# Removal key's inverse norm in a recurrent mixer: token-major power on GpSimd and four transposes, in place of logarithm and exponential on ScalarE

## The chip, the cores and the metric

One core of one Trainium2 chip runs the whole kernel. Its engines work side by side, each through its own queue in order: TensorE (PE: matrix products into PSUM), VectorE (DVE), ScalarE (ACT), GpSimd (POOL, which does not touch PSUM here) and SyncE (SP, which issues the weight loads). The metric is the device time of one execution in microseconds (us). The three timed runs gave 1562.68, 1556.77 and 1562.52 us: median 1562.52 us.

## The reference, cut to what matters

Two layers of attention branches are followed by two layers of a second kind. In each of these, three mixers work on the same input of 256 tokens and 1024 features: gated linear attention, an RWKV-7 recurrence (4 heads of 64 features) and sparse attention; an output projection, a layer norm and a feed-forward network follow. The change is in the recurrence, in the normalised key that the state forgets by (the removal key `kk`):

```python
kk = (k * k_k).reshape(B, S, H, N)                      # H = 4 heads, N = 64
kk = kk / jnp.maximum(jnp.sqrt(jnp.sum(kk * kk, axis=-1, keepdims=True)), 1e-12)
...
xs = (heads(r), heads(decay), heads(k), heads(v),
      (-kk).transpose(1, 0, 2, 3), (kk * a_h).transpose(1, 0, 2, 3))
def step(state, inp):
    r_t, w_t, k_t, v_t, a_t, b_t = inp
    sa = jnp.einsum('bhvk,bhk->bhv', state, a_t)
    state = (state * w_t[:, :, None, :] + sa[..., None] * b_t[:, :, None, :]
             + v_t[..., None] * k_t[:, :, None, :])
    return state, jnp.einsum('bhvk,bhk->bhv', state, r_t)
```

## The kernel before, in words

Feature-major tiles hold 256 features as 128 partitions x 2 column groups x 256 tokens, so that a partition's two groups belong to two different heads and a head covers 64 partitions. The recurrence (`rwkv`, line 897) is worked out in closed form over chunks, not step by step. For the norm (lines 939 to 952) ACT squares `k * k_k` in two halves (L941), PE multiplies each half by `c_ones64`, a 128x128 matrix of two blocks of ones, which leaves each head's sum on all its 64 partitions (L944), DVE clips it at 1e-24 (L946), ACT takes the logarithm (L947) and the exponential of minus half of it (L949), and DVE multiplies the key by the result (L952, whose records carry L301, the line of the helper `stt`). In the trace the squares' tile is `kk`, the clipped sum and its inverse root `ssg`, the normalised key `kn`.

From `kn` DVE makes the operands of the recurrence (`r_AR`, `r_B`, `ke`, `r_K`: lines 954 to 970). PE sums r x k per head (L975) and later starts the chunk's triangular inverse (L1014).

The four streams of a layer (recurrence, gated linear attention, direct and compressed sparse attention) are generators that `side_by_side` (line 210) draws from in turn by the numbers that they yield. Each instruction gets a priority, shifted by the table `AHEAD`; a scheduler then writes one fixed order for each engine, so that the recurrence's instructions stand between those of the others. In the stretch of the norm these are

- L353: the projection of the gated linear attention, 128x512 products in full fp32 (two records each in the trace);
- L656 and L659: scores of the direct attention and their mask; L595, L597, L601: row maximum, its negative and the exponentials; L446: transposes of the probabilities (and of everything else that `transposed` turns over); L610: their copy to `ptsb`; L613: the weighing of the values by them; L438: a filler product;
- L1356 to L1382: the compressed attention's hidden layer. Its PSUM bank (`psg`, one buffer) is free for L1379 only when DVE has made `n_hid` (L1372).

PE's order and each other engine's are fixed when the kernel is built; at run time an engine waits at the head of its queue until its operands are there. PSUM for the recurrence comes from `psr`, a pool of one pair of banks that are handed out in turn.

A power on GpSimd stands elsewhere already: L890 (128x8, in `head_norm`), L479 and L499 (128x1, in the row norms).

Of the kernel before, what the change touches and what calls it, by code (L numbers as in the profile page):

```python
# [8 lines left out]
F32 = mybir.dt.float32  # L9
F32R = mybir.dt.float32r  # L10
BF16 = mybir.dt.bfloat16
AF = mybir.ActivationFunctionType
ALU = mybir.AluOpType
# [138 lines left out]
class Kern:  # L152
    def __init__(self, ctx, tc, ap):
        self.tc, self.nc, self.ap = tc, tc.nc, ap
        pool = lambda n, b, **k: ctx.enter_context(tc.tile_pool(name=n, bufs=b, **k))
        self.cp = pool("const", 1)
        self.wh = pool("whi", 4)
        self.wl = pool("wlo", 4)
        self.wr = pool("raw", 5)
        self.sm = pool("small", 4)  # L160
        self.pp, self.pr = (pool(n, 1, space=PSUM) for n in ("pp", "pr"))
        self.rest = {}
        self.turn = 0
        self.last = self.pr
        self.slot = 0
        nc = self.nc
        self.c = {}
        const = lambda n, w, v: (lambda t: (nc.vector.memset(t, v), t)[1])(self.cp.tile([128, w], F32, name=n))
        self.one = const("one", 1, 1.0)
        self.mhalf = const("mhalf", 16, -0.5)  # L170
        self.ln10 = const("ln10", 1, float(10 * np.log(2.0)))
        warm = self.cp.tile([128, 1], F32, name="warm")
        nc.scalar.activation(warm, self.one, AF.Square)

# [722 lines left out]
    def rwkv(self, l, R, wa, g0, tl, P, hp, rows, out):  # L897

        nc = self.nc
        mm = nc.tensor.matmul  # L900
        r, k, v = R["r"], R["k"], R["v"]
        cst = self.c
# [26 lines left out]
        if l:  # L929
            tv = self.tanh_half(self.low_rank(self.psr, P, P_TAIL, 32, 64, tl), hp[:, 4:6])  # L930
            d = self.c3("vd")
# [7 lines left out]
        sq = self.c3("kk2")  # L939
        for c in range(2):  # L940
            nc.scalar.activation(sq[:, c], k[:, c], AF.Square, scale=P[:, P_KK + c:P_KK + c + 1])  # L941
        ss = self.psr(2, 256)
        for c in range(2):
            mm(ss[:, c], cst["ones64"], sq[:, c], start=c == 0, stop=c == 1)  # L944
        sg = self.c3("ssg")
        nc.vector.tensor_scalar(sg, ss, 1e-24, None, op0=ALU.max)  # L946
        nc.scalar.activation(sg, sg, AF.Ln, scale=float(2.0 ** 20))  # L947
        rn = sg
        nc.scalar.activation(rn, sg, AF.Exp, scale=-0.5, bias=self.ln10)  # L949
        kn = self.c3("kn")  # L950
        for c in range(2):
            self.stt(kn[:, c], k[:, c], P[:, P_KK + c:P_KK + c + 1], rn[:, c], ALU.mult, ALU.mult)  # L952
# [19 lines left out]
        for tt in range(2):  # L972
            for c in range(2):
                o = 4 * tt + 2 * c
                mm(bp[:, o:o + 2], rk[:, c, 128 * tt:128 * tt + 128], P[:, P_RK + 2 * c:P_RK + 2 * c + 2],  # L975
                   start=tt == 0 and c == 0, stop=tt == 1 and c == 1)
# [35 lines left out]
        for n, j, b in quads:  # L1012
            tt, c = tiles[n]
            mm(ps[half[b], j, n], ar4[tt][half[j], 0, c, half[b]], Bt[half[j], c, 128 * tt + 64 * b:128 * tt + 64 * b + 64],  # L1014
               start=n == 0, stop=n == 3)
# [44 lines left out]
        for q in range(1, 6):  # L1060
            ps, idle = pair()
            for n, j, b in quads:
                tt, c = tiles[n]
# [30 lines left out]
        for tt in both:  # L1094
# [4 lines left out]
            for h in range(4):  # L1099
                j, c = hh(h)  # L1100
# [3 lines left out]
            for h in range(4):  # L1104
                j, c = hh(h)
# [3 lines left out]
            for h in range(4):  # L1109
                j, c = hh(h)  # L1110
# [11 lines left out]
        for h in range(4):  # L1122
            j, c = hh(h)
# [22 lines left out]
        for tt in range(2):  # L1146
            yield 3
            tm, M, WU, V = tiles[tt]
            if tt:
                pw = self.psr(2, 128)  # L1150
                for h in range(4):
                    j, c = hh(h)
# [4 lines left out]
            for h in range(4):  # L1157
                j, c = hh(h)
# [327 lines left out]
    def block2_layer(self, l, xT):  # L1486
# [48 lines left out]
        def rwkv():  # L1535
            for t in self.rwkv(l, R, wa, g0, tl, P, hp, rows, yr):
                yield t
            with self.sec("ofr"):
                feats["r"] = self.out_feat([yr[:, 0], yr[:, 1]], 0.5, self.psr)

        self.side_by_side([(0, "rwkv", rwkv()), (AHEAD["t_gla"], "gla", gla()), (AHEAD["t_dir"], "nsa", direct()), (AHEAD["t_cmp"], "cmp", compressed())])
        with self.sec("h1"):
            for n in range(2):
# [257 lines left out]
```

## Time and profile before

| what | us |
|---|---|
| three timed runs | 1562.68, 1556.77, 1562.52 (median 1562.52) |
| the profiled execution's own time | 1556.73 |
| its span | 1554.9 |
| PE busy | 1492.6 (96%) |
| PE weight load busy | 1286.2 (83%) |
| DVE busy | 938.9 (60%) |
| ACT busy | 710.6 (46%) |
| POOL busy | 50.0 (3%) |

The span is the profiled execution from its first to its last record; 1.8 us of its own time lie around it. Busy times are sums over instructions, and PE's ends are modelled, so its share says where PE had work, not that it ran at its peak. The granted clock is a share of full speed (2.4 GHz); its mean over the span is 0.988. The two stretches of the norm lie at about 775 to 790 us (first layer) and 1205 to 1220 us (second layer).

### The profile page before, as it was taken

The page shows a single profiled execution, that of the slowest core. Times are in us where ns is not written, and L with a number is a line of the kernel's source. Part 1 is how long each engine was busy: PE and PEld are TensorE (multiplying, and loading weights), DVE is VectorE, ACT ScalarE, POOL GpSimd, SP SyncE. Part 2 cuts the span into 40 slices and gives each one's busy share as a digit, 9 for nine tenths or more (in the row PEclk, how much of TensorE's full clock was granted, in tenths as well). Part 3 has the DMA queues.
Part 4 walks back from the last instruction along what each step waited for, and adds up shares of the span by engine and source line. Part 5 has one row for each costly group of instructions (what it writes and reads, how often), then busy time and mean ns, then how long its engine had stood idle before and what let it go on. Part 6 is the DMA issues. An engine that isn't in the chain of part 4 may idle for free.

```text
span 1554.9 us, 26032 instructions
## 1 busy us (share of the span) xinstructions
PE 1492.6 (96%) x10502; PEld 1286.2 (83%) x10502; DVE 938.9 (60%) x1531; ACT 710.6 (46%) x1286; POOL 50.0 (3%) x82
## 2 busy tenths in 40 slices
PE   6999999999999999999999989999999999899997
PEld 5877899988787999868767769998888677789986
DVE  5586565565686655565367475556754675755564
ACT  5545554445454444444454334444454544344451
POOL 0000000000000000000011010000000010100000
PEclk9999999999999999999999999999999999999999
DMA  7743435445444445556710245556447101445560
GB/s 254 235 147 122 150 122 189 158 156 180 166 149 131 149 136 182 167 152 201 249 34 2 80 142 176 188 172 224 139 146 254 42 1 42 144 164 191 181 215 27
DMA packets 72984, 231.69 MB, mean 149 GB/s; under 512 B 8736, under 2 KB 11552, under 8 KB 72864
## 3 DMA queue, kind: packets, MB, share of 16 engines
q1 hardware_dynamic: 67248, 219.74, 42.8%
q10 hardware_dynamic: 5616, 10.30, 2.1%
q8 instruction: 82, 1.34, 0.3%
q14 instruction: 38, 0.31, 0.1%
HBM read 228.96 MB, written 1.05 MB: 148 GB/s over the span
## 4 chain that ended last, share of the span: by engine, by line
PE 46%; DVE 4%; DMA 3%; ACT 2%; issue 1%; POOL 0%; DVEq 0%; ACTq 0%; SPq 0%
PE ps L357 10%; PE ps L355 10%; PE ps L356 10%; PE ps L353 4%; DMA raw<-in_stream_dram 2%; PE ps L446 2%; PE ps L1258 2%; PE ps L613 1%; PE ps L656 1%; DVE wlo L298 1%; ACT whi L321 1%; PE ps L438 1%; PE ps L867 1%; PE ps L1052 0%; PE ps L1001 0%
## 5 line engine op out<-in xcount | busy, mean ns | idle before, releaser
L298 DVE TENSOR_TENSOR wlo<-raw,whi 128x1024 fp32r<-128x1024 f32 (+2 forms) x364 | 428.1, 1183 | 313.3 <-ACT whi L321 306.2
L321 ACT CAST whi<-raw 128x1024 fp32r<-128x1024 f32 (+2 forms) x364 | 367.8, 1018 | 403.9 <-PE ps L356 206.4
L355 PE MATMUL ps<-xTh,whi 128*128 128x256 f32 x720 | 205.5, 285 | 4.4 <-ACT whi L321 4.4
L357 PE MATMUL ps<-xTh,wlo 128*128 128x256 f32 x720 | 205.5, 285 | 1.5 <-DVE wlo L298 1.5
L356 PE MATMUL ps<-xTl,whi 128*128 128x256 f32 x720 | 205.1, 285 | 0.0
L357 PE MATMUL ps<-hTh,wlo 128*128 128x256 f32 x640 | 182.4, 285 | 0.0
L355 PE MATMUL ps<-hTh,whi 128*128 128x256 f32 x640 | 181.7, 284 | 0.0
L356 PE MATMUL ps<-hTl,whi 128*128 128x256 f32 x640 | 181.5, 284 | 0.0
L355 PEld LDWEIGHTS ps<-xTh,whi 128*128 128x128 f32 x720 | 138.8, 193 | 6.1 <-ACT whi L321 4.8
L357 PEld LDWEIGHTS ps<-xTh,wlo 128*128 128x128 f32 x720 | 138.8, 193 | 2.0 <-DVE wlo L298 1.9
L356 PEld LDWEIGHTS ps<-xTl,whi 128*128 128x128 f32 x720 | 138.7, 193 | 0.8
L356 PEld LDWEIGHTS ps<-hTl,whi 128*128 128x128 f32 x640 | 122.6, 191 | 1.1 <-issue 0.7
L355 PEld LDWEIGHTS ps<-hTh,whi 128*128 128x128 f32 x640 | 122.6, 192 | 0.7
L357 PEld LDWEIGHTS ps<-hTh,wlo 128*128 128x128 f32 x640 | 122.6, 192 | 0.4 <-issue 0.3
L355 PE MATMUL ps<-whi,hTh 128*128 128x512 f32 (+2 forms) x256 | 97.3, 380 | 1.1 <-ACT wi L772 1.1
L357 PE MATMUL ps<-whi,hTl 128*128 128x512 f32 (+2 forms) x256 | 97.0, 379 | 0.0
L356 PE MATMUL ps<-wlo,hTh 128*128 128x512 f32 (+2 forms) x256 | 95.9, 375 | 0.8 <-DVE wlo L298 0.8
L355 PE MATMUL ps<-whi,xTh 128*128 128x512 f32 (+1 forms) x144 | 55.1, 383 | 4.0 <-ACT xTh L425 2.5
L355 PEld LDWEIGHTS ps<-whi,hTh 128*128 128x128 f32 x256 | 48.1, 188 | 11.8 <-issue 3.3
L355 PE MATMUL ps<-whi,f_h 128*128 128x512 f32 x144 | 57.1, 396 | 0.0
L356 PE MATMUL ps<-wlo,f_h 128*128 128x512 f32 x144 | 57.0, 396 | 0.0
L357 PE MATMUL ps<-whi,f_l 128*128 128x512 f32 x144 | 56.9, 395 | 0.0
(474 smaller groups left out, 2898.1 us busy)
## 6 DMA issues: line engine op xcount, KB each, us to landing
raw<-in_stream_dram SPq DMA_DIRECT2D x346, 512.0 KB, 4.2
raw<-in_stream_dram SPq DMA_DIRECT2D x56, 256.0 KB, 3.1
whi<-in_stream_dram SPq DMA_DIRECT2D x11, 512.0 KB, 5.9
wlo<-in_stream_dram SPq DMA_DIRECT2D x11, 512.0 KB, 6.5
row<-in_ln_w_dram ACTq DMA_DIRECT2D x8, 256.0 KB, 4.0
row<-in_ln_b_dram ACTq DMA_DIRECT2D x8, 256.0 KB, 4.6
raw<-in_stream_dram SPq DMA_DIRECT2D x4, 480.0 KB, 3.8
raw<-in_stream_dram SPq DMA_DIRECT2D x4, 420.0 KB, 5.4
```

The lines of the kernel that those rows point to most:

```text
L298: self.nc.vector.tensor_tensor(out=out, in0=a, in1=b, op=op)
L321: nc.scalar.copy(hi[:, :b - a], raw)
L353: mm(out, a, b, start=start, stop=stop)
L355: mm(out, a[0], b[0], start=start, stop=False)
L356: mm(out, a[0], b[1], start=False, stop=False)
L357: mm(out, a[1], b[0], start=False, stop=stop)
L438: self.nc.tensor.matmul(o, self.negb, self.causb[:, None, :].to_broadcast([128, n, 128]), start=True, stop=True)
L446: self.nc.tensor.transpose(pt[:, j], s, self.ident)
L613: nc.tensor.matmul(o[:, ocol(h)], ps[:, i * nk + k, :], vt(k, h), start=first and i == 0 and k == 0, stop=last and i == nh - 1 and k == nk ...
L656: nc.tensor.matmul(s3[:, i], qT[pr, h // 2], kT(pr, h, 128 * nk), start=i == 0, stop=False)
L867: self.nc.tensor.matmul(ps[:, c], P[r0:r1, off + 128 * c:off + 128 * c + 128], rhs[r0:r1], start=c == 0, stop=c == 1)
L1258: mm(ps[:, tt, c], a, e, start=tt + c == 0, stop=c == 1 and (tt == 1 or m == 128))
```

## The change

The squares stay feature-major. PE now takes them as the stationary operand, 128 tokens at a time, against two columns of `c_ones64` (the first of each block): four products of 128x2, which leave the heads' sums token-major, 128 tokens x (2 token tiles x 2 groups x 2 heads) = 128x8. DVE clips these 8 columns, POOL raises them to the power -0.5 in one 128x8 instruction, DVE spreads each of the values over 64 columns in two copies of 128x256 into the tile of the squares, and four transposes on PE bring that back to feature-major, into a PSUM bank (`rn`), from which DVE multiplies the key. The logarithm, the exponential, the tile `ssg` and the constant `ln10` go.

```diff
-        self.ln10 = const("ln10", 1, float(10 * np.log(2.0)))
...
-        ss = self.psr(2, 256)
+        ss = self.psr(2, 2, 2)
+        for tt in range(2):
+            for c in range(2):
+                mm(ss[:, tt, c], sq[:, c, 128 * tt:128 * tt + 128], cst["ones64"][:, ::64], start=tt + c == 0, stop=tt + c == 2)
+        s8 = self.sm.tile([128, 2, 8], F32, name="r_s8")
+        nc.vector.tensor_scalar(s8[:, 0], ss.rearrange("p t c j -> p (t c j)"), 1e-24, None, op0=ALU.max)
+        nc.gpsimd.tensor_tensor(out=s8[:, 1], in0=s8[:, 0], in1=self.mhalf[:, 0:8], op=ALU.pow)
+
+        rn = self.psr(2, 256)
+        for tt in range(2):
+            wide = sq[:, tt].rearrange("p (c j d) -> p c j d", c=2, j=2)
+            nc.vector.tensor_copy(wide, s8[:, 1, 4 * tt:4 * tt + 4].rearrange("p (c j) -> p c j", c=2)[:, :, :, None].to_broadcast([128, 2, 2, 64]))
         for c in range(2):
-            mm(ss[:, c], cst["ones64"], sq[:, c], start=c == 0, stop=c == 1)
-        sg = self.c3("ssg")
-        nc.vector.tensor_scalar(sg, ss, 1e-24, None, op0=ALU.max)
-        nc.scalar.activation(sg, sg, AF.Ln, scale=float(2.0 ** 20))
-        rn = sg
-        nc.scalar.activation(rn, sg, AF.Exp, scale=-0.5, bias=self.ln10)
+            for tt in range(2):
+                nc.tensor.transpose(rn[:, c, 128 * tt:128 * tt + 128], sq[:, tt, 128 * c:128 * c + 128], self.ident)
         kn = self.c3("kn")
```

In the changed file the helpers' lines stand one lower (L445 is the transposes' L446, L612 the weighing's L613, L352 the projection's L353), the new sums are L944, the new clip L946, the power L947, the copies L952, the transposes L955, and lines behind them stand six higher.

PE in the first layer, from the new sums to the weighing, before:

```order
L446 MATMUL ps<-c_ident,pexp 128x128 x4
L944 MATMUL ps<-kk_7914,c_ones_6935 128x256
L353 MATMUL ps<-whi,xTf 128x512
L656 MATMUL ps<-n_kw,n_qT 128x128
L613 MATMUL ps<-n_vs_7043,ptsb 128x64 x4
L1364 MATMUL ps<-c_fold,n_Xl 128x30 x2
L656 MATMUL ps<-n_kw,n_qT 128x128
L944 MATMUL ps<-kk_7914,c_ones_6935 128x256
L656 MATMUL ps<-n_kw,n_qT 128x128 x2
...
L438 MATMUL ps<-causb,negb 128x512
L446 MATMUL ps<-c_ident,pexp 128x128 x4
```

The same place on PE in the changed kernel (`kk` is the squares' tile under L944 and the spread inverse norm under L955):

```order
L445 MATMUL ps<-c_ident,pexp 128x128 x4
L944 MATMUL ps<-c_ones_6933,kk_7912 128x2
L352 MATMUL ps<-whi,xTf 128x512 x2
L612 MATMUL ps<-n_vs_7041,ptsb 128x64 x4
L1370 MATMUL ps<-c_fold,n_Xl 128x30 x2
L944 MATMUL ps<-c_ones_6933,kk_7912 128x2 x3
L655 MATMUL ps<-n_kw,n_qT 128x128 x4
...
L437 MATMUL ps<-causb,negb 128x512
L955 MATMUL ps<-c_ident,kk_7912 128x128
L445 MATMUL ps<-c_ident,pexp 128x128
L955 MATMUL ps<-c_ident,kk_7912 128x128 x3
L1385 MATMUL ps<-n_hidk,P_7022 128x32 x2
```

The four scores L656 stand together behind the sums now, and the new transposes stand in the filler's and the probabilities' wake, five rows (with mask and filler) behind the last sum; one more projection product stands ahead of the sums, and L1379 (now L1385) moves up to right behind the transposes. In the second layer the order is the same but for two probability transposes, not one, between the first new transpose and the other three.

DVE in the second layer, before:

```order
L298 TENSOR_TENSOR yn<-ps,n_cf 128x512
L946 TENSOR_SCALAR ssg<-ps 128x512
L1367 TENSOR_SCALAR n_x_11999<-n_x_11999 128x60
L595 TENSOR_REDUCE mx<-ps 128x4
L298 TENSOR_TENSOR n_x_11999<-n_x_11999,ps 128x60
L597 TENSOR_SCALAR nb<-mx 128x4
```

And in the changed kernel:

```order
L297 TENSOR_TENSOR yn<-ps,n_cf 128x512
L946 TENSOR_SCALAR r_s_12020<-ps 128x8
L1373 TENSOR_SCALAR n_x_12004<-n_x_12004 128x60
L952 COPY kk_12012<-r_s_12020 128x256
L297 TENSOR_TENSOR n_x_12004<-n_x_12004,ps 128x60
L952 COPY kk_12012<-r_s_12020 128x256
L594 TENSOR_REDUCE mx<-ps 128x4
L300 SCALAR_TENSOR_TENSOR n_hidv<-n_x_12004,ps 128x4x15
L300 SCALAR_TENSOR_TENSOR kn<-r_k,P_11114,ps 128x256 x2
L596 TENSOR_SCALAR nb<-mx 128x4
```

The copies, which wait for POOL, stand ahead of the row maximum and, in the second layer, one of them ahead of the product for `n_x`; in the first layer that product stands ahead of both copies. No instruction of the weight stream stands between the clip and the copies.

ACT in the first layer, before:

```order
L1366 ACTIVATE n_x_7906<-ps 128x60
L947 ACT_TABLE_LOAD
L947 ACTIVATE ssg<-ssg 128x512
L1369 ACT_TABLE_LOAD
L1369 ACTIVATE n_x_7906<-n_x_7906 128x60
L949 ACTIVATE ssg<-ssg,ln_80 128x512
L601 ACTIVATE pexp,n_den<-ps,nb 128x128 x4
L1382 ACTIVATE n_kc<-ps 64x15 x2
```

And in the changed kernel:

```order
L1372 ACTIVATE n_x_7904<-ps 128x60
L1375 ACTIVATE n_x_7904<-n_x_7904 128x60
L1388 ACTIVATE n_kc<-ps 64x15 x2
L600 ACTIVATE pexp,n_den<-ps,nb 128x128 x4
```

Two table loads and two activations of 128x512 go in each layer; no other table load of the program moves.

## Rows read from the trace of the kernel before

**Rows 1.** Windows, both stretches: length, busy (count) per engine, granted clock, DMA share, GB/s.
```profile
770.00:800.00 30.00, 30.00 (x160) 18.42 (x159) 12.54 (x26) 17.14 (x49) 3.55 (x8) 1.00 0.22 70
1200.00:1230.00 30.00, 30.00 (x192) 18.64 (x190) 15.51 (x30) 17.71 (x50) 2.79 (x6) 1.00 0.16 55
```

**Rows 2.** Chain that ended last, first layer: start us, us on the chain, what.
```profile
772.58 1.09 PE ps L656 x8
...
776.80 0.43 PE ps L944 x2
777.24 0.86 PE ps L353 x2
778.10 0.42 PE ps L656 x2
778.51 1.03 PE ps L613 x8
779.55 0.42 PE ps L1364 x4
779.96 0.42 PE ps L656 x2
780.38 0.63 PE ps L944 x2
781.01 0.64 PE ps L656 x4
781.65 0.32 PE ps L659
781.97 0.22 PE ps L438
782.18 0.44 PE ps L446 x4
...
789.08 0.84 PE ps L613 x8
...
794.26 0.79 PE ps L975 x8
...
825.29 0.84 PE ps L1229 x8
```

**Rows 3.** Timeline of ACT: start us, us, line, operation.
```profile
780.24 1.28 ACT L947 ACT_TABLE_LOAD   x1
...
786.85 0.59 ACT L610 COPY ptsb<-ps 128x512 f32<-128x512 f32 x1
```

**Rows 4.** Timeline of POOL: powers of 128x8.
```profile
880.31 1.68 POOL L890 TENSOR_TENSOR hn<-hn,mhalf 128x8 f32<-128x8 f32 x1 [49.63 <-DVE hn L889]
...
898.94 2.57 POOL L890 TENSOR_TENSOR hn<-hn,mhalf 128x8 f32<-128x8 f32 x1 [4.95 <-DVE hn L889]
```

**Rows 5.** Timeline of DVE: the clip, the products behind it, and beside the powers.
```profile
781.05 0.69 DVE L946 TENSOR_SCALAR ssg<-ps 128x512 f32<-128x512 f32 x1 [0.60 <-PE ps L944]
...
791.47 0.69 DVE L298 TENSOR_TENSOR ke<-r_r,ke 128x512 f32<-128x512 f32 x1
...
880.07 0.17 DVE L889 TENSOR_SCALAR hn<-hn 128x8 f32<-128x8 f32 x1
880.39 0.69 DVE L298 TENSOR_TENSOR n_t<-ps,n_cf 128x512 f32<-128x512 f32 x1 [0.16 <-PE ps L613]
...
898.76 1.22 DVE L298 TENSOR_TENSOR wlo<-raw,whi 128x1024 fp32r<-128x1024 f32 x1
```

**Rows 6.** Groups by line and form: busy us, mean ns | idle before.
```profile
L1103 DVE COPY r_WU<-ps 64x256 f32<-64x256 f32 x2 | 0.8, 418 | 1.6 <-PE ps L1102 1.6
...
L479 POOL TENSOR_TENSOR rs<-ms,mhalf 128x1 f32<-128x1 f32 x10 | 5.5, 552 | 539.3 <-DVE ms L477 539.3
```

**Rows 7.** Windows, second layer behind the norm, columns as in rows 1.
```profile
1230.00:1246.00 16.00, 13.77 (x154) 10.35 (x146) 12.39 (x34) 5.36 (x16) 1.40 (x2) 1.00 0.10 34
1246.00:1254.00 8.00, 7.33 (x25) 4.79 (x26) 4.20 (x11) 4.25 (x9) 1.09 (x1) 0.57 0.00 0
```

## The prediction

> **What bounds the kernel now.** I read the page first (PE is busy nearly all the span, every other engine far less), then the place of the change: the windows of the two stretches, the chain of waits through them, the timelines of ACT, DVE and POOL there, and last the windows of the clock. In both stretches, 30 us each, PE is busy 30.00 of 30.00 us at the full granted clock, ACT 17 to 18, DVE 13 to 16, POOL about 3 [rows 1]. The chain of waits agrees: from the first sum (776.80 us) to the weighing (789.08) and on to L975 (794.26) it stays on PE without a gap [rows 2]. So in this stretch a microsecond counts only if PE does more or less work, or if PE is made to wait. What ACT saves counts only through an operand that PE waits for, and PE waits for none here.
>
> **What ACT loses.** Two table loads in each layer, of 1.28 us as the first of them [rows 3], and the logarithm and exponential with them. PE is on the chain throughout, so I price all of it at nothing. What hides it is the projection L353, of which PE still has eight pieces after the first probabilities. If that cover were gone, the copy L610, which ends at 786.85 + 0.59 = 787.44, 1.6 us ahead of its reader at 789.08 [rows 2, 3], would be the first to profit.
>
> **PE's own work, per layer.** Between the first sum and the probability transposes PE does, besides the projection, L944 0.43 + 0.63, L656 0.42 + 0.42 + 0.64, L613 1.03, L1364 0.42, L659 0.32 and L438 0.22: 4.53 us [rows 2]. In the new order the sums are four products of two columns. Their nearest row is L1229, the same form, eight records in 0.84. The scores stand in one piece as at 772.58 (1.09), and L613 no longer follows a score: 0.84 as at 789.08 [rows 2]. With L1364, L659 and L438 as they are: 0.84 + 1.09 + 0.84 + 0.42 + 0.32 + 0.22 = 3.73, so 0.80 less. The four transposes cost what four cost at 782.18, 0.44 [rows 2]. Net PE work: -0.36 us. Most of that saving is the order's (scores no longer split in three), not the smaller sums'.
>
> **The new wait, per layer.** PE now meets transposes that depend on a trip through three engines. From the end of the last sum: 0.04 us to DVE (L944's end at 781.01, the clip's start at 781.05 [rows 2, 5]), the clip of eight columns 0.17 as L889, 0.07 to POOL (880.24 to 880.31), the power 1.68 [rows 4, 5], 0.04 back, the first copy of 256 columns 0.42 as L1103 [rows 6], 0.05 to PE: 2.47 us. What PE has in the meantime is the scores, mask and filler: 1.09 + 0.32 + 0.22 = 1.63 us. PE stands for 0.84 us. Then the second copy: its result is some 0.3 us behind the first's, PE has one (first layer) or two (second) probability transposes and its own in between, 0.11 each; in the second layer a product for `n_x` also stands between the copies. I put 0.14 on it in both. Stall 0.98, work -0.36: +0.62 us per layer, **+1.2 us** for both.
>
> What is queued behind: on PE everything, since its order is fixed, the probability transposes and then L353. On DVE the row maximum and `n_hidv` wait behind the copies, which wait for POOL; L1379 needs `n_hidv`'s bank, and it now stands right behind the transposes. The tanh in front of `n_hidv` is no longer behind two table loads, so I count it in time, at nothing; if it isn't, PE waits a few tenths.
>
> **The power's price** is the one that decides. Two durations of the 128x8 form stand in the trace, 1.68 and 2.57 [rows 4]; the 128x1 form takes 0.55 [rows 6]. Beside the long one DVE was in the middle of `wlo` (128x1024, from 898.76), beside the short one it worked on `n_t`, with one operand in PSUM [rows 5]. In the new order nothing of the weight stream stands between clip and copies; beside the power DVE has a small product and then waits. So I take 1.68, and keep both ends: at 0.55 the whole trip (1.34 us) lies under the 1.63 and the layer gains 0.36; at 2.57 the stall is 1.87 and the layer loses 1.51. For two layers: -0.7 to +3.0 us.
>
> The Trainium skill ("SBUF — State Buffer", section "Who interferes with whom") states that a DVE instruction with two SBUF inputs and a GpSimd instruction that reads SBUF exclude each other for the whole instruction. The pair of rows agrees (2.57 beside `wlo`, 1.68 beside `n_t`), and by that rule too the new power is a short one, because the DVE product beside it reads PSUM.
>
> The skill's "GPSIMD Engine Reference" (section "Elementwise — side-by-side cycle accounting") has GpSimd about half as fast as VectorE on a two-input elementwise operation. By that the power would be an estimated 0.34 us, twice the clip's 0.17, and the trip would be hidden; the trace's 1.68 speaks against it, ten times the clip, so the sum goes by the trace and the rule's outcome is the first rival below.
>
> **Behind the stretch.** PE would reach the first transpose at 776.80 + 3.73 + 1.72 (two projection products at 0.86, one more than before) + 0.84 = 783.09, and the weighing that needs L610 after the transposes of both kinds (0.88), 0.14, L1379 (about 0.4) and eight projection pieces (8 x 0.43): 787.95. L610 ended at 787.44 before, and I expect it within a few tenths of that: its exponentials lose the wait for the tables and gain one for the copies. L975 is then reached at 787.95 + 0.84 + 3.44 = 792.23 instead of 794.26, since two products moved behind it. Its operand was ready at 791.47 + 0.69 = 792.16 [rows 5]. I take no wait, but there is no cushion left: should DVE run half a microsecond later, it is +0.5 per layer, +1.0 in all.
>
> All else shifts with PE: there is no gap in the chain to absorb it, and I see no transfer that limits this stretch (DMA share 0.22 and 0.16 [rows 1]).
>
> **Rivals.**
>
> 1. *Hidden.* The power is fast enough, or the order leaves more cover than I count. For it: POOL is idle and DVE quiet. Against it: no 128x8 power shorter than 1.68 in the rows shown. Price -0.7 us: 1561.8.
> 2. *The clock.* Behind the second layer's norm the granted clock was 0.57 over eight microseconds [rows 7]: most of them at the lower level (1.2 GHz), after 16 us in which PE was busy for 13.77 only, at full clock. Full-speed work lost there: 8 x (1 - 0.57) = 3.4 us. That stretch now begins somewhat later, and the dip may not come: +1.2 - 3.4 = -2.2, so 1560.3. The three runs of one program, 5.9 us apart, show that something of this size comes and goes anyway.
> 3. *Slower.* The power takes its long form in both layers, PE idles 1.9 us per layer ahead of the stretch in which it has gaps anyway, and the clock falls once more in each layer: 3.0 + 2 x 3.4 = +9.8 us, 1572.3. For it: the dip after a stretch with gaps [rows 7]. Against it: PE is at 30.00 of 30.00 around the new wait, and a gap of one to two microseconds stands alone there. It decides from a power of about 2.5 us on.
> 4. *The change doesn't do what it says:* the loads come back elsewhere. The order shows four fewer and no new one, so this is all but excluded; it would cost ACT, not PE: still +1.2.
>
> **How the numbers follow.** The sum is made against the profiled execution (own time 1556.73 us, span 1554.9), which stands with the lowest of the three runs (1556.77) and 5.8 us below their median. +1.2 makes 1557.9 there, and on the median 1562.52 + 1.2 = 1563.7 us, which I give. Chances: the forecast 0.60, hidden 0.12, the clock's gain 0.14, slower 0.10, other 0.04. The range: from a run at the lower level with the trip hidden (1556.77 - 0.7 = 1556.1, a little less for its own spread) to the long powers and late L975 with half a dip on top (1562.68 + 3.0 + 1.0 + 1.7 = 1568.4, a little more): 1555.5 to 1569. Half a per cent, about what a measurement of this kernel can tell from no change, is 7.8 us. The forecast and rivals 1 and 2 lie within it; faster by more would need two dips to vanish together (0.06); rival 3 makes slower, less the part in which it costs under 7.8 (0.09); the same 0.85.
>
> **What would show it.** In the changed kernel's chain: the new sums eight records in 0.84 and the scores one piece in 1.09; a gap on PE of 0.7 to 1.1 us ahead of the first L955 in both layers, released by DVE's copy, and that by a POOL record of about 1.7 us; ACT without table loads there; L975 reached within 0.5 us of its operand. I am wrong if PE has no gap there (the trip is hidden), if the gap is near 2 us (the long power), if L975 or L1379 shows a wait above half a microsecond, or if the time moves by more than 4 us with the granted clock unchanged.

## The result, and the profile after

The changed kernel takes 1566.53 us on the median of 20 runs (1557.19 to 1572.40); the kernel before, run beside it, 1555.67 (20 runs, 1551.49 to 1562.68). The ratio is 1.0062, 95% interval 1.0046 to 1.0079: slower by 7 to 12 us. A second measurement, in another session, gave 1.0039 (1.0010 to 1.0068). The forecast was +1.2 us, 1563.7 us on the median. The 1566.53 us lie within the forecast range of 1555.5 to 1569, but only because the 1562.52 us to which the +1.2 was added were high: over 20 runs the kernel before took 1555.67.

| | before | after |
|---|---|---|
| profiled execution's own time, us | 1556.73 | 1562.58 |
| its span, us | 1554.9 | 1560.8 |
| mean granted clock of the span | 0.988 | 0.982 |
| PE busy, us | 1492.6 | 1500.3 |
| ACT busy, us | 710.6 | 704.2 |

Where the norm stands, the profile after looks as forecast. First the windows that answer to [rows 1]; columns as there.

```profile
770.00:800.00 30.00, 29.13 (x183) 18.67 (x183) 14.82 (x36) 14.29 (x51) 4.68 (x9) 1.00 0.16 51
1200.00:1230.00 30.00, 29.02 (x161) 18.09 (x161) 14.16 (x30) 13.96 (x45) 3.44 (x7) 1.00 0.19 66
```

PE, busy for 30.00 of 30.00 us before, now lacks 0.87 and 0.98. The chain that ended last shows why; in the first layer it leaves PE for DVE and POOL where it had stayed on PE [rows 2]. Columns: start us, us on the chain, what.

```profile
775.95 0.42 PE ps L1370 x4
776.37 0.66 PE ps L944 x6
777.03 0.02 issue
777.05 0.18 DVE r_s L946
777.23 0.07 issue
777.31 1.69 POOL r_s L947
778.99 0.02 issue
779.02 0.31 DVE kk L952
779.32 0.14 issue
779.46 0.30 PE ps L955
...
784.36 0.84 PE ps L612 x8
785.20 3.49 PE ps L352 x8
788.68 0.79 PE ps L981 x8
```

From the end of the last sum to the first transpose are 2.43 us, of which the power is 1.69. Beside them PE had the scores in one piece, the mask and a filler. Its own timeline has the wait in brackets (start us, us, engine, line, operation, tiles, shape, count), here the first layer and then the second:

```profile
776.21 0.81 PE L944 MATMUL ps<-c_ones,kk 128*128 128x2 f32 x6
776.95 1.16 PE L655 MATMUL ps<-n_kw,n_qT 64*128 64x128 f32 x8
778.03 0.39 PE L658 MATMUL ps<-causb,negb 128*128 128x512 bf16 x1
778.26 0.38 PE L437 MATMUL ps<-causb,negb 128*128 128x512 bf16 x1
779.46 0.30 PE L955 MATMUL ps<-c_ident,kk 128*128 128x128 f32 x1 [0.82 <-DVE kk L952]
...
1213.65 0.33 PE L955 MATMUL ps<-c_ident,kk 128*128 128x128 f32 x1 [0.98 <-DVE kk L952]
```

Behind it nothing new waits. The copy to `ptsb` on ACT, which answers to the second of [rows 3], and `ke` on DVE, which answers to the second of [rows 5], are early:

```profile
782.68 0.60 ACT L609 COPY ptsb<-ps 128x512 f32<-128x512 f32 x1
```
```profile
786.87 0.69 DVE L297 TENSOR_TENSOR ke<-r_r,ke 128x512 f32<-128x512 f32 x1
```

Their readers on PE start at 784.36 and 788.68, 1.1 us behind the end of each. From the probability transposes to the chunk's inverse the first layer takes 25.10 us instead of 24.48 (+0.62, as forecast), the second 24.55 instead of 23.67 (+0.88). That is 1.5 us, and the kernel lost more.

The rest is in the clock. PE's windows behind the norm (length, busy, granted clock, DMA share, GB/s), first of before, then of after:

```profile
810.00:820.00 10.00, 8.99 (x116) 1.00 0.01 2
820.00:830.00 10.00, 10.00 (x123) 1.00 0.01 2
830.00:840.00 10.00, 10.00 (x133) 1.00 0.01 2
1240.00:1250.00 10.00, 9.00 (x105) 0.84 0.01 2
1250.00:1260.00 10.00, 10.00 (x95) 0.82 0.01 2
1260.00:1270.00 10.00, 10.00 (x131) 1.00 0.01 2
```
```profile
810.00:820.00 10.00, 9.00 (x70) 0.81 0.01 2
820.00:830.00 10.00, 10.00 (x70) 0.50 0.00 0
830.00:840.00 10.00, 10.00 (x117) 0.84 0.01 2
1240.00:1250.00 10.00, 8.04 (x106) 0.98 0.01 2
1250.00:1260.00 10.00, 10.00 (x38) 0.50 0.00 0
1260.00:1270.00 10.00, 10.00 (x93) 0.50 0.01 2
```

Twice, some 36 us behind the end of PE's new wait, the clock goes to its lower level (1.2 GHz) and stays there for 17 and 20 us. "PE busy" says nothing of it: 10.00 of 10.00 either way, but 38 records instead of 95. The same products of 128x64 in before and in after:

```profile
821.39 2.00 PE L1052 MATMUL ps<-r_tm,r_M 128*128 128x64 f32 x16
```
```profile
820.35 3.67 PE L1058 MATMUL ps<-r_tm,r_M 128*128 128x64 f32 x16
```

Up to the fall PE does the same products with the same waits as before, 3.0 us earlier in this pair of profiles; behind it it is 4.8 us late: 7.8 us in one place. The second layer's fall costs 6.2. Before has shorter falls of its own: none in this stretch of the first layer, 6.8 us in the second's, others elsewhere.

How far that carries over many runs shows in the runs of the kernel before, each listed with its mean granted clock: over 115 of them (four sessions, beside the experiments) time = 1539.3 + 1455 x (1 - clock) us, with a correlation of -0.97. Their mean clock is 0.9861. In the 32 runs of after it is 0.9818: 0.0043 x 1455 = 6.2 us of a difference in these means of 6.5 (the 20 runs of before in the first session, whose median was lower, have no clocks listed). Two of the 115, at 1571.57 and 1573.92 us, are counted as slow and stand outside the ratios; without them the line is 1539.4 + 1449 x (1 - clock) and the mean clock 0.9862. So the clock is most of the loss, and what is left for the direct cost is below the trace's 1.5.

### The profile page after: what moved, and what is told of

It reads as the page before. It is cut to its first block, busy times and chain, and to the rows that moved or that the text cites. A ratio compares the mean times of both kernels' runs of the same rounds, so it can differ in the third digit from the quotient of the medians.

```text
span 1560.8 us, 26058 instructions
## 1 busy us (share of the span) xinstructions
PE 1500.3 (96%) x10518; PEld 1293.5 (83%) x10518; DVE 938.2 (60%) x1534; ACT 704.2 (45%) x1278; POOL 51.5 (3%) x84
## 4 chain that ended last, share of the span: by engine, by line
PE 42%; issue 5%; DVE 4%; DMA 3%; ACT 2%; POOL 1%; DVEq 0%; ACTq 0%; POOLq 0%
PE ps L356 9%; PE ps L354 9%; PE ps L355 9%; PE ps L352 3%; DMA raw<-in_stream_dram 2%; PE ps L445 2%; PE ps L1264 2%; PE ps L612 1%; PE ps L655 1%; DVE wlo L297 1%; ACT whi L320 1%; PE ps L437 1%; PE ps L1058 1%; PE ps L1007 1%; DVE dn L300 0%
## 5 line engine op out<-in xcount | busy, mean ns | idle before, releaser
L297 DVE TENSOR_TENSOR wlo<-raw,whi 128x1024 fp32r<-128x1024 f32 (+2 forms) x364 | 428.2, 1184 | 308.0 <-ACT whi L320 299.6
```

Of the source, the lines that this page charges most:

```text
L297: self.nc.vector.tensor_tensor(out=out, in0=a, in1=b, op=op)
```

## The experiments

Three theories. **S**: PE's wait ahead of the new transposes brings the clock down behind it. **P**: only the moment at which the later stretch arrives decides, whatever shifted it. **C**: chance of the runs. Later a fourth, **W**: the new form of PE's work (two-column sums, other order) does it. "Low" in this table counts runs with a mean clock of 0.983 or less, a line drawn only for counting; wait is PE's ahead of the new transposes in the two layers, by the profile. The ratios are to the runs of before in the same session; before's mean clock was 0.9857 beside again, fill4, shift4 and alone, 0.9863 beside nopow, pow2, keepA and keepB, 0.9857 beside nofill4, keepA1 and keepB1, and 0.9869 beside alone2.

| kernel | wait, us | ratio to before (95%) | mean clock | low |
|---|---|---|---|---|
| before | none | 1 | 0.9861 | 32 of 115 |
| after, first | 0.82, 0.98 | 1.0062 (1.0046 to 1.0079) | 0.9820 | 14 of 20 |
| again | 0.81, 0.98 | 1.0039 (1.0010 to 1.0068) | 0.9814 | 11 of 12 |
| fill4 | none, 0.55 | 1.0027 (0.9988 to 1.0066) | 0.9844 | 5 of 12 |
| shift4 | none | 0.9971 (0.9941 to 1.0002) | 0.9874 | 0 of 12 |
| alone | 0.69, 0.83 | 1.0014 (0.9984 to 1.0045) | 0.9856 | 3 of 12 |
| nopow | none | 0.9989 (0.9958 to 1.0020) | 0.9858 | 5 of 12 |
| pow2 | 2.25, 2.59 | 1.0054 (1.0029 to 1.0080) | 0.9819 | 9 of 12 |
| nofill4 | none | 1.0005 (0.9969 to 1.0042) | 0.9861 | 3 of 12 |
| keepA | 0.82, 0.98 | 1.0004 (0.9980 to 1.0029) | 0.9891 | 0 of 12 |
| keepB | none | 0.9964 (0.9936 to 0.9992) | 0.9908 | 0 of 12 |
| keepA1 | 0.81, 0.98 | 1.0014 (0.9989 to 1.0039) | 0.9872 | 0 of 12 |
| keepB1 | none | 0.9968 (0.9942 to 0.9994) | 0.9905 | 0 of 12 |
| alone2 | 2.30, 2.44 | 1.0052 (1.0024 to 1.0079) | 0.9847 | 3 of 12 |

**again**: the changed kernel, unaltered.

> The changed kernel once more, for a second profile. Measured so far: 1.0062 of before (interval 1.0046 to 1.0079), some 9.7 us, of which the two stretches of the norm hold 0.6 and 0.9 us by the two profiles and the rest lies where the granted clock is at its lower level: 17 and 20 us behind the norms against 0 and 7 before. Theory S (the gap on PE at the new transposes brings the clock down later) and theory P (nothing of the change but when the later work arrives decides the clock): both expect +8 to +11 us and again two long stretches at the lower level. Theory C (chance: the two profiles drew different luck): the profile shows one long stretch or none, and the mean clock of the runs is that of the runs of before.

1566.78 us. The lower clock is there again, in 11 of 12 runs. So it is no chance of one session: C falls by the runs. The profile alone would not have said so, since it has one long fall where S expected two: none behind the first layer's norm. In this profile the clock also falls at PE's wait itself, in both layers (the first wait ends at 787.67, the second at 1221.14 us); windows as above:

```profile
780.00:786.00 6.00, 6.00 (x48) 1.00 0.29 94
786.00:794.00 8.00, 7.19 (x22) 0.57 0.01 2
1212.00:1220.00 8.00, 8.00 (x59) 1.00 0.23 68
1220.00:1224.00 4.00, 3.02 (x11) 0.57 0.00 0
1250.00:1258.00 8.00, 6.99 (x102) 1.00 0.01 2
1258.00:1278.00 20.00, 20.00 (x129) 0.50 0.00 1
```

**fill4**: the changed kernel with four filler products of 512 columns ahead of the transposes.

```diff
         rn = self.psr(2, 256)
+        self.busy("kk", rn.rearrange("p c t -> p (c t)"))
...
-KEEP = dict(lev=2,
+KEEP = dict(kk=4, lev=2,
```

> The changed kernel with four filler products (128x512 bf16, 0.22 us each, nothing reads them) on PE ahead of the first new transpose: the wait for the power is filled with work, the transposes stand at nearly the same time (0.1 us later). Theory S: without the gap the clock stays up behind the norms and the time is before + 1.5 to 2.5 us (about 1558). Theory P: the work behind arrives as in the changed kernel, so the time is that of the changed kernel within 2 us (about 1566), with long stretches at the lower clock.

1564.82 us, clock between the two. The wait is gone in the first layer, but 0.55 us of it is left in the second, since the order of the other instructions moved too:

```profile
1212.28 0.87 PE L956 MATMUL ps<-c_ident,kk 128*128 128x128 f32 x4 [0.55 <-DVE kk L953]
```

Behind the first layer's norm the fall is short (3.4 us), behind the second's it lasts 20.5 us as in after. That fits S, but the interval reaches from no change to the full loss.

**shift4**: the kernel before, with the four fillers ahead of its first sum.

```diff
         ss = self.psr(2, 256)
+        self.busy("kk", ss.rearrange("p c t -> p (c t)"))
```

> The kernel before with four filler products of 0.22 us on PE ahead of the first sum of each layer: no power, no wait, logarithm and exponential kept; everything behind comes 0.9 us later, which is what the change does to the second layer (0.6 in the first). Theory S: +1.8 us (8 x 0.22) and the clock of before. Theory P: the clock behind the norms changes as it does with the change, +6 to +11 us.

The fillers take PE 0.87 us. From the probability transposes to the chunk's inverse the layers take 25.03 and 24.23 us, 0.56 more than in before (after: 0.62 and 0.88 more), and nothing of the loss shows: 0.9971, clock 0.9874. A delay alone does not do it, which is against P.

**alone**: the kernel before, with the new chain beside its own (clip, power, copies, four transposes whose result nobody reads).

```diff
+        nc.vector.tensor_scalar(s8[:, 0], ss[:, 1, 0:8], 1e-24, None, op0=ALU.max)
+        nc.gpsimd.tensor_tensor(out=s8[:, 1], in0=s8[:, 0], in1=self.mhalf[:, 0:8], op=ALU.pow)
...
+                nc.tensor.transpose(xx[:, c, 128 * tt:128 * tt + 128], wd[:, tt, 128 * c:128 * c + 128], self.ident)
         rn = sg
```

> The kernel before with the new chain beside it and unused: eight columns of the sums are clipped, raised on GpSimd, spread by two copies and turned over by four transposes that nothing reads; logarithm, exponential and the sums of before stay. The transposes stand one projection product behind the probability transposes, and their data comes an estimated 0.7 us after PE is there: a gap on PE in each layer, +0.44 us of transposes, +2.2 us in all. Theory S: the gap brings the clock down, +8 to +11 us. Theory P: +2.2 us, and beside it whatever 1.1 us per layer does to the clock, which need not be a loss.

Here PE waits nearly as long as in after, 0.69 and 0.83 us, and its sums and scores have before's form. The wait stands a little further on, behind the probability transposes and one projection product:

```profile
783.45 0.66 PE L958 MATMUL ps<-c_ident,kk 128*128 128x128 f32 x4 [0.69 <-DVE kk L955]
...
1218.55 0.74 PE L958 MATMUL ps<-c_ident,kk 128*128 128x128 f32 x4 [0.83 <-DVE kk L955]
```

The clock stays at 0.9856, within 0.0005 of before. The time is 1564.07 us, 5.4 above before on the medians and 3.2 on the means, where 2.2 were expected for the direct cost and 8 to 11 by S. So S as it was put, any wait here is enough, fails; W came in. It speaks against P too: the chunk's inverse comes 1.35 and 1.57 us later than in before.

**nopow**: the changed kernel with the power left out; the clip, now with an upper bound of 0.001, writes straight into the columns that are spread. The removal key then has other values, and so has all that the recurrence makes of it.

```diff
-        nc.vector.tensor_scalar(s8[:, 0], ss.rearrange("p t c j -> p (t c j)"), 1e-24, None, op0=ALU.max)
-        nc.gpsimd.tensor_tensor(out=s8[:, 1], in0=s8[:, 0], in1=self.mhalf[:, 0:8], op=ALU.pow)
+        nc.vector.tensor_scalar(s8[:, 1], ss.rearrange("p t c j -> p (t c j)"), 1e-24, 1e-3, op0=ALU.max, op1=ALU.min)
```

> The changed kernel with the power left out: the clip, now with an upper bound of 0.001, writes the values that the copies spread, so GpSimd is out of the trip and the removal key has another length. PE's instructions and their order are those of the changed kernel. Trip: 2.47 - 1.68 - 0.07 = 0.72 us, under PE's cover of 1.63, so the gap of 0.82 and 0.98 us ahead of the new transposes goes; directly that is -0.9 us per layer against the changed kernel, so about 0 to -0.7 us against before. Theory S (the gap on PE brings the granted clock down some 35 us later): mean granted clock back from 0.982 to about 0.987, time within 2 us of before. Rival P (only the moment at which the later stretch arrives decides, the gap does not matter): the stretch arrives 0.9 us per layer earlier, the clock may be anything from 0.980 to 0.988. Rival W (the other form of PE's work, sums of two columns and the new order, brings the clock down): clock stays at 0.982, time 6 to 8 us above before.

PE's order is that of after, and the wait is gone; the same place as above, second layer:

```profile
1218.64 1.16 PE L655 MATMUL ps<-n_kw,n_qT 64*128 64x128 f32 x8
1219.73 0.39 PE L658 MATMUL ps<-causb,negb 128*128 128x512 bf16 x1
1219.95 0.38 PE L437 MATMUL ps<-causb,negb 128*128 128x512 bf16 x1
1220.17 0.27 PE L954 MATMUL ps<-c_ident,kk 128*128 128x128 f32 x1
```

The clock returns to 0.9858 and the time to 0.9989 of before: the new form without the wait loses nothing, against W. One rival stays open, that the other values, and not the missing wait, bring the clock back. No run has the new form with the norm's own values and no wait in both layers; the nearest is the first layer of fill4, whose fall is 3.4 us. What remains of chance shows too: this one profile has a 20.5 us fall behind the first layer's norm, with no wait ahead of it. If the wait makes such falls likelier, it is not their only cause.

**pow2**: the power taken twice, the first result unused.

```diff
+        nc.gpsimd.tensor_tensor(out=s8[:, 2], in0=s8[:, 0], in1=self.mhalf[:, 0:8], op=ALU.pow)
         nc.gpsimd.tensor_tensor(out=s8[:, 1], in0=s8[:, 0], in1=self.mhalf[:, 0:8], op=ALU.pow)
```

> The changed kernel with the power taken twice, one behind the other (the first result is not used): PE's gap ahead of the new transposes grows by one power, from 0.82 and 0.98 us to about 2.5 and 2.7 us. Directly +3.4 us against the changed kernel for both layers. Theory S: more of the same, mean granted clock at or under 0.982, time 11 to 16 us above before. Rival P: the stretch arrives 1.7 us per layer later, the clock may come back to 0.987, time about 5 us above before. Rival W: clock as in the changed kernel, 0.982, time 11 us above before.

```profile
785.59 0.45 PE L956 MATMUL ps<-c_ident,kk 128*128 128x128 f32 x1 [2.25 <-DVE kk L953]
...
1219.96 0.48 PE L956 MATMUL ps<-c_ident,kk 128*128 128x128 f32 x1 [2.59 <-DVE kk L953]
```

The wait grows by 3.0 us in all, the clock stays where it was (0.9819) and the time is 9.6 us above before, under the 11 to 16 forecast by S. Here the loss in clock did not grow with the wait.

**nofill4**: nopow (again without the power), with the four fillers of fill4 where PE had waited.

```diff
         rn = self.psr(2, 256)
+        self.busy("kk", rn.rearrange("p c t -> p (c t)"))
...
-KEEP = dict(lev=2,
+KEEP = dict(kk=4, lev=2,
```

> The changed kernel with the power left out (as in nopow) and, in place of PE's wait, four filler products of 512 columns (0.86 us together) ahead of the new transposes: the later stretch arrives as late as in the changed kernel, but PE never waited. Without the power the trip is 0.72 us, under the cover, so no gap. Theory S (the gap makes a long fall of the granted clock likelier): mean clock over the runs 0.985 to 0.988, as before and as without the power, time 0 to 4 us above before (0.6 to 0.9 us per layer are direct). Rival P (the moment of arrival decides): clock as in the changed kernel, 0.981 to 0.982, time 7 to 9 us above before.

The fillers put back most of the time that PE waited (four products, 1.04 us busy in the second layer; the chunk's inverse comes 0.45 and 0.39 us later than in before, against after's 0.62 and 0.88), and PE does not wait:

```profile
1214.48 1.04 PE L437 MATMUL ps<-causb,negb 128*128 128x512 bf16 x4
1215.36 0.60 PE L955 MATMUL ps<-c_ident,kk 128*128 128x128 f32 x4
```

1560.00 us beside 1559.79 of before, clock 0.9861. Work in place of the wait costs 0.2 us on the median (the interval reaches from -0.3 to +0.4%); the changed kernel with the wait lost 8.1 (again) and 10.9. With shift4 and alone this leaves little of P: delays of 0.4 to 0.6 and of 1.4 to 1.6 us per layer, on either side of after's 0.62 and 0.88, all leave the clock at 0.9856 or above. A moment that does harm only between them is not excluded.

**keepA and keepB**: after and before, each with four fillers at two places of the later stretch, where PE waits in after as in before: 0.95 to 0.98 us for the transposed block probabilities (`n_pT`) and 1.00 us for `r_P`. In after's second layer the 1.00 us end at 1248.44, and the long fall begins 1.2 us later:

```profile
1248.44 0.66 PE L445 MATMUL ps<-c_ident,r_P 128*128 128x128 f32 x4 [1.00 <-DVE r_P L297]
```

```diff
             oc = self.psg(2, 4, 64)
+            self.busy(f"oc{tt}", oc.rearrange("p g h d -> p (g h d)"))
...
-            nc.scalar.copy(q, self.transposed(self.psr, [Pm[:, n].rearrange("p j k -> p (j k)") for n in range(4)])
+            nc.scalar.copy(q, self.transposed(self.psr, [Pm[:, n].rearrange("p j k -> p (j k)") for n in range(4)], f"tp{rd}")
...
-KEEP = dict(lev=2,
+KEEP = dict(oc0=4, oc1=0, tp0=0, tp1=4, tp2=0, tp3=0, tp4=0, lev=2,
```

> The changed kernel with four filler products of 512 columns (0.21 us each) put at two places per layer in the stretch behind the norm where PE waited 0.95 to 0.98 us for the transposed block probabilities and 1.00 us for r_P. The gap ahead of the new transposes stays. If the 7 us that are not the direct cost lie in the low granted clock behind these two gaps (17.1 us at half the clock from 816 us on, 20.5 us from 1250 us on), these falls go: mean granted clock 0.987 to 0.990, time 1 to 3 us above before. If the low clock there does not hang on these gaps, the clock stays near 0.982 and the time 7 to 10 us above before (the fillers themselves cost up to 0.3 us per place where they do not fit).

> The kernel before with the same fillers at the same two places per layer as the changed kernel with fillers. Its own falls there (6.8 us at half the clock from 1246.7 us on in the profiled run) should go in the same way: 0 to 4 us faster than before, mean granted clock 0.988 to 0.992. The difference between the two kernels with fillers should then be the direct cost alone, 1.5 us, if the rest is the low clock behind these gaps; 7 us or more if it is not.

1558.91 and 1553.81 us: clock 0.9891 and 0.9908, no low run in either, and no fall behind the norm in either profile. So the long falls and the low runs hang on that stretch. The distance between the two norms does not go with them: 5.1 us on the medians (3.7 on the means) are left, where 1.5 had been expected if the stretch held the rest of the loss and 7 if it did not. The means of the clock still differ by 0.0017, 2.5 us of the 3.7.

**keepA1 and keepB1**: the same with the fillers at the second place alone.

```diff
-KEEP = dict(lev=2,
+KEEP = dict(oc0=0, oc1=0, tp0=0, tp1=4, tp2=0, tp3=0, tp4=0, lev=2,
```

> The changed kernel with the fillers at only one of the two places, ahead of the second transposes of r_P, where PE waited 1.00 us per layer. At the other place the fillers had waited with the products behind them and cost 0.8 us per layer, so this should be some 1.6 us faster than the kernel with both, if the one place is enough to keep the clock (0.988 to 0.990): 0 to 1 us under before on the median, no more than 2 us above. If both places were needed, the clock is 0.982 to 0.985 and the time 4 to 8 us above before.

> The kernel before with the fillers at that one place alone. If the one place is enough: mean clock 0.990 to 0.992, 4 to 7 us under before, and 1 to 4 us faster than the changed kernel with the same fillers (1.5 us direct and what the gap ahead of the transposes still costs in clock). If not: as before, clock 0.986 to 0.987.

1562.20 and 1554.59 us. One place is enough against the long falls (no low run), but not as I had put it. The fillers close no wait: they meet it themselves, and stand as work behind it (keepA1, second layer):

```profile
1252.95 1.02 PE L437 MATMUL ps<-causb,negb 128*128 128x512 bf16 x4 [1.00 <-DVE r_P L297]
1253.82 0.60 PE L445 MATMUL ps<-c_ident,r_P 128*128 128x128 f32 x4
```

In keepA1 the clock still falls at the wait at the norm, in the second layer (the wait ends at 1216.59):

```profile
1208.00:1216.00 8.00, 7.61 (x57) 1.00 0.20 68
1216.00:1220.00 4.00, 3.41 (x11) 0.57 0.00 0
```

keepA1 was expected up to 1 us under before, at most 2 above, with a clock of 0.988 to 0.990; it came out 2.4 us above on the median, at 0.9872. It is 7.6 us above keepB1 (6.8 on the means, of which the clock's 0.0033 make 4.8), where 1 to 4 had been expected: with no low run in either, nearly all of the loss is there again. Both kernels with fillers in before's form beat before and after; the new norm loses in either pair.

**alone2**: alone with the power taken twice.

```diff
+        nc.gpsimd.tensor_tensor(out=s8[:, 2], in0=s8[:, 0], in1=self.mhalf[:, 0:8], op=ALU.pow)
         nc.gpsimd.tensor_tensor(out=s8[:, 1], in0=s8[:, 0], in1=self.mhalf[:, 0:8], op=ALU.pow)
```

> The kernel before with the unused chain beside it (clip, power, two copies, four transposes of nothing that is read), now with the power taken twice: PE's gap ahead of the added transposes grows from 0.69 and 0.83 us to some 2.3 and 2.5 us, while PE's own sums and scores keep the form of before. Directly +3.3 us against the chain with one power, some +6 us against before at the same clock. If a gap there is enough by itself once it is long: mean granted clock 0.981 to 0.983, time 10 to 13 us above before. If it takes the new form of PE's work (two-column sums, new order) together with a gap, as it looks by now (without a power 0.986, with the chain in before's form 0.986, both together 0.982): clock stays at 0.985 to 0.987, time 5 to 8 us above before.

The waits are 2.30 and 2.44 us, and the clock is 0.9847, 0.0022 under before in the same session: 3.2 us of the 8.5 between the means. That lies between the two expectations. The two forms of PE's work seem to answer differently to a wait even this long (3 low runs of 12, against 9 of 12 in pow2 in another session), though this profile has the long fall in the second layer; twelve runs each do not settle it.

The profiles of the kernels without the later fillers side by side, second layer, behind the second transposes of `r_P`: the clock is at its lower level for some 20 us in after, again, fill4, pow2 and alone2 (waits 0.98, 0.98, 0.55, 2.59, 2.44); for under 7 us in before and shift4, not at all in nopow and nofill4 (no wait), and not at all in alone (0.83). The first layer does not show that: a long fall in after (17.1 us) and in nopow, which has no wait there (20.5 us), and 3.4 us or none in the eight others without the later fillers, four of which wait 0.69 to 2.30 us. In both layers together these ten kernels have a long fall behind six of 11 waits and behind one of 9 places without.

Of the 15 waits of 0.55 us and more in all the profiles, five have a fall that begins in the wait's last 0.7 us (again twice, pow2, alone2, keepA1), and one more fall, in the first layer of pow2, begins 0.5 us ahead of the wait; at the 13 places without a wait, none does.

## Why the prediction was right or wrong

- **PE's work and the trip: right.** The power took 1.68 and 1.65 us (1.68 taken), the clip 0.17, the sums and the single piece of scores stand as forecast, and the gap of 0.82 us in the first layer answers to 0.84. +0.62 us was forecast for each layer; 0.62 and 0.88 were measured in the two stretches. The short price of the power held in both layers. The reason given for it, that DVE's product beside the power reads PSUM, was not put to the test: DVE had next to nothing beside it. In the first layer the product for `n_x` (L297 at 777.14, 0.21 us) ends 0.04 us into the power; in the second it stands behind the first copy. In both DVE is idle for 1.7 us ahead of the copies, here the first layer:

```profile
779.02 0.50 DVE L952 COPY kk<-r_s 128x256 f32<-128x256 f32 x2 [1.67 <-POOL r_s L947]
```

- **What ACT loses at nothing: right.** Without power and wait, nopow is level with before (0.9989, 0.9958 to 1.0020): two table loads fewer in each layer buy nothing that these runs can tell.
- **No wait behind: right, and safer than I said.** Operands of the weighing and of r x k were there 1.1 us ahead in the first layer, where I saw no cushion for L975; in the second PE shows no wait at either.
- **"All else shifts with PE": wrong, and this is the step that failed.** I let the stretch behind the norm run at the clock that it had before, so the clock's loss stood in the sum at nothing. The mean clock of the runs went from 0.9861 to 0.9818, 6.2 us, five times the +1.2 that I had worked out. In the profile of after the loss lies in that stretch (7.8 and 6.2 us); that it lies there in all runs is not shown (keepA1).
- **The number: luck, in part.** 1563.7 came within 2.8 us of 1566.53 because two errors met: the start was 6.9 us too high (1562.52 from three runs, 1555.67 from twenty) and the forecast loss 9.7 us too small. The signs named for the new sums, the gap, the power and ACT came true (only r x k came 1.1 us behind its operand, not within 0.5), and none of the signs of being wrong did, since none of them asked for a lower clock.
- **Rival 3 was mis-built.** It had the mechanism, PE idles ahead of a stretch with gaps and the clock falls in each layer, and nearly the price (+9.8 us), with a chance of 0.10. But it let this decide only from a power of about 2.5 us on, since "a gap of one to two microseconds stands alone there". In the new form 0.82 and 0.98 us were enough, with the short power, and 1.4 and 1.6 us more of it (pow2) changed the clock no further. **Rival 2** read the same dip the other way round: a later arrival might spare it. shift4 and nofill4 show that a shift of half a microsecond does not bring the loss; that it gains anything is not shown (shift4: no low run, but 0.9971 with an interval up to 1.0002).

Shown by runs: the loss is nearly all clock (again, after), and in the new form it is gone where PE's wait is gone (nopow, nofill4). More work in the later stretch removes the long falls and the low runs (keepA, keepB, keepA1, keepB1), but not the distance between the two norms. Not settled: whether the other values in nopow and nofill4 have a part in it; and why nearly the same wait in before's form of the work (alone, alone2) costs less clock. There a wait and the new form together do what neither does alone, and no run separated the two-column sums from the changed order or from the place of the wait.

## What to carry to other kernels

A wait put on PE where it had none is to be priced twice: its length on the chain, and what the granted clock does in the next stretch in which PE already has gaps; here the second was four times the first. Compare the mean granted clock over many runs before explaining a difference by instructions: two profiles of one kernel differed by 11.5 us here (1560.8 and 1572.3). Work in the wait's place cost nothing that could be measured in nofill4, where the power was left out too; with the power kept (fill4) one wait of 0.55 us stayed, and the interval reaches from no loss to the full one. In before's form 0.86 us of fillers per layer in the later stretch bought 5 us on the medians (1 to 9 by the interval); with the new norm the same fillers left the kernel 2.4 us above before (keepA1).

## What was not expected of the hardware

- PE at 10.00 of 10.00 us busy with the granted clock at 0.50 for 20 us on end, behind waits of 1.0 us or less each. That it falls at all behind them was known from [rows 7]; that it stays so long with PE busy was not.
- The clock's answer did not grow with the wait in these runs: in the second layer 0.55, 0.98 and 2.59 us brought the same 20 us at the lower level in fill4, after and pow2, and after and pow2 have the same mean clock (0.9818, 0.9819).
- The kernel before is at the edge as well: 32 of its 115 runs have a mean clock of 0.983 or less, and these have a median near 1567 us, as after; with 0.86 us of fillers per layer behind the second `r_P` wait none is left (keepB1: 0 of 12).
